# A hybrid decoder layer: the norm weights' row loaded first, one filter ordered behind scans, small products regrouped by array shape

## The chip, the cores and the metric

One core of a Trainium2 chip runs the whole program. The core has five engines that work at the same time and wait for each other by semaphores: TensorE (PE in the profile, its weight loads PEld), VectorE (DVE), ScalarE (ACT), GpSimd (POOL) and SyncE (SP), which here only issues DMA transfers. The metric is the device time of one execution in microseconds; the number given for a kernel is the median of its runs. Three runs of the kernel before took 1643.97, 1646.79 and 1654.39 us.

## The reference

One inference step of one decoder layer, for a prompt of 1024 positions and for 8 x 8 = 64 sample tokens; D_MODEL is 1024. All is in float32. The input projection feeds three groups of heads whose outputs are concatenated:

```python
h = rmsnorm(x, lw['g_mix'])
proj = h @ lw['w_in']
p_rw, p_cv, p_sb = jnp.split(proj, [RW_PROJ, RW_PROJ + 3 * CONV_DIM], axis=-1)
...
# recurrence (4 heads of 64), state s is 64 x 64 for each head
sa = jnp.einsum('bhvk,bhk->bhv', s, a_t)
s = (s * w_t[:, :, None, :] + sa[..., None] * b_t[:, :, None, :]
     + v_t[..., None] * k_t[:, :, None, :])
y = jnp.einsum('bhvk,bhk->bhv', s, r_t)
...
# short convolution, a filter of three taps
u = pc * px
ext = jnp.concatenate([conv_prev.astype(u.dtype), u], axis=1)
y = conv_w[0] * ext[:, 0:T]
for j in range(1, CONV_K):
    y = y + conv_w[j] * ext[:, j:j + T]
return pb * y, ext[:, -(CONV_K - 1):]
...
# stick-breaking attention (8 heads of 64)
log_beta = jnp.where(mask, jax.nn.log_sigmoid(z), -jnp.inf)
log_keep = jnp.where(mask, jax.nn.log_sigmoid(-z), 0.0)
later = lax.cumsum(log_keep, axis=3, reverse=True) - log_keep
wts = jnp.exp(log_beta + later)
...
x = x + mixed @ lw['w_out']
h2 = rmsnorm(x, lw['g_mlp'])
x = x + jnp.square(jax.nn.relu(h2 @ lw['w_up'])) @ lw['w_down']
gate = jax.nn.sigmoid(rmsnorm(x, lw['g_ple']) @ lw['w_ple_gate'])
x = x + gate * (p @ lw['w_ple_proj'])
```

The outputs also hold the new keys and values, the recurrence's final states, the last projection rows and the last two convolution inputs, for the prompt and for the samples.

## The kernel before

The code is one function that is traced from top to bottom. A planner then writes the order of each engine's instructions: it plays the program through with costs of its own, and takes at every engine the first instruction in program order that is ready in that play. So a line that stands earlier in the program has precedence, but does not always come first. Two calls restrict the planner: `tc.keep_in_program_order(x)` holds an instruction to its place in the program on its engine, and `with tc.issue_after(y)` puts what is traced inside it behind the instruction `y` on `y`'s engine. On the chip each engine and each DMA queue runs its list strictly in order. Buffers are named slots: `bufs=n` says how many tiles of a name live at once, and a tile that takes a used slot waits for the slot's last reader.

A float32 matrix product is split in two: a value is cast to a rounded format (fp32r, "hi"), the rest is kept as "lo", and three products of the parts are added. The recurrence and the transposes use plain float32, and each plain float32 product stands as two records in the profile.

**Stage 1, norm and transposes (lines 94 to 218, up to 38 us).** `x_tile` (L106) loads x in nine tiles of up to 128 rows through six slots. The row of norm weights (`gbc`, L113, 4 KB) is spread over 128 partitions by a product with ones (L120) and copied back (L121). For each tile: sum of squares (ACT, L205), root (L206), reciprocal (DVE, L208), scaling by it and the weights (DVE, L209), eight transposes (PE, L214), cast (ACT, L216), remainder (DVE, L217). The first input weights `w_da` are loaded before this loop; their casts are on ACT (L156) and their remainders on POOL (L159). Eleven rows of parameters (`prow`, L200) are loaded from POOL's queue; L223 transposes them into `par`, and L353 uses them. SP also carries small loads: `wl2` (L308 to L310), `sh` (L319), `gains` and `gainT` (L328, L330), `bias` (L791).

**Stage 2, recurrence inputs (to 150 us).** `rw_tile` makes the projections of the recurrence by `gemm_t` (L171 to L173, chunks of 384, 384 and 320 positions) and prepares products for its chunks of 64 positions.

**Stage 3, recurrence beside attention's projections (150 to 420 us).** Two streams of `wkv_local` work on pairs of chunks (`e` is 0 or 1, the chunk in the pair). L535 multiplies, for each `e`, `j` and half `s` of the partitions, a 64 x 128 stationary block by 128 columns; `s` 0 and 1 write two banks. Later products in it (L559 to L600) have 64 x 64 blocks. `wkv_chain` takes the pairs in order: L648 and L656 have 128 x 64 blocks and do not need the state; L659 and L665 have 64 x 64 blocks and need the state of the chunk before. For each chunk it goes L656, L659 for the first two heads, then L656, L659 for the other two, then L665. All of these lie between the dense products of the attention's projections (L898) and of the convolution (L171 to L173), which fill PE.

**Stage 4, samples, convolution and attention's first half (420 to 545 us).** `wkv_sample_chunk` does the samples' recurrence. `convolution` makes three projections; between the second and the third, for each half `j` of its columns, the filter runs as one ACT instruction (L1049) and two DVE instructions over 1104 columns (L1050, L1052). The third projection's result is multiplied by the filter's result as it leaves its bank (L1069); it has two banks. `attention` makes units, each a head and 256 queries: scores (PE, L954, L955), two sigmoids (ACT, L956, L957), masks (POOL, L961), scan (DVE, L963), product (DVE, L965), transposes (L979) and values (L983). Convolution and attention are traced in turns, five steps of the one and four of the other; `marks[1]` is the scan traced last.

**Stage 5, output projection, MLP, gate (545 us to the end)** is not touched.

## Time and profile before

| | |
|---|---|
| median of three runs | 1646.79 us |
| profiled execution | 1648.17 us |
| its span, first to last instruction | 1646.5 us |
| PE busy | 1617.9 us (98%) |
| DVE busy | 988.6 us (60%) |
| ACT busy | 774.2 us (47%) |
| POOL busy | 713.8 us (43%) |

The profiled execution is 1.4 us above the median. A line of the timeline has the start in us, the length in us of a group of like instructions, the engine, the line of the code, the operation, its output and inputs, their shapes, and the number of records. In square brackets stand idle time before it and what ended that. A matmul's length reaches into the next one's, since matmuls are pipelined, so that for PE the distance from one start to the next says more than the length. A row of windows has for each stretch the busy time of PE, PEld, DVE, ACT and POOL with the count of instructions, then the granted clock of PE and the DMA share.

### The profile page before, as it was taken

The page shows a single profiled execution, that of the slowest core. Times are in us where ns is not written, and L with a number is a line of the kernel's source. Part 1 is how long each engine was busy: PE and PEld are TensorE (multiplying, and loading weights), DVE is VectorE, ACT ScalarE, POOL GpSimd, SP SyncE. Part 2 cuts the span into 40 slices and gives each one's busy share as a digit, 9 for nine tenths or more (in the row PEclk, how much of TensorE's full clock was granted, in tenths as well). Part 3 has the DMA queues.
Part 4 walks back from the last instruction along what each step waited for, and adds up shares of the span by engine and source line. Part 5 has one row for each costly group of instructions (what it writes and reads, how often), then busy time and mean ns, then how long its engine had stood idle before and what let it go on. Part 6 is the DMA issues. An engine that isn't in the chain of part 4 may idle for free.

```text
span 1646.5 us, 28968 instructions
## 1 busy us (share of the span) xinstructions
PE 1617.9 (98%) x11215; PEld 1402.2 (85%) x11215; DVE 988.6 (60%) x1692; ACT 774.2 (47%) x1502; POOL 713.8 (43%) x793
## 2 busy tenths in 40 slices
PE   6999999999999999999999999999999999999998
PEld 5999777778976777777777789979999999999897
DVE  6367644554467698776344462478776777768332
ACT  7643245333356676665444452474433433437321
POOL 6321202232354664444256614467644554539110
PEclk9999999999999999999999999999999999999999
DMA  5245555434436534332356662223322222223211
GB/s 173 92 134 162 152 134 148 107 101 118 128 111 195 170 99 136 105 109 80 100 185 206 179 208 89 79 65 104 102 90 90 87 81 90 91 78 95 69 47 42
DMA packets 188148, 190.60 MB, mean 116 GB/s; under 512 B 57450, under 2 KB 147338, under 8 KB 187884
## 3 DMA queue, kind: packets, MB, share of 16 engines
q1 hardware_dynamic: 173644, 165.37, 33.6%
q0 software_dynamic: 5472, 16.81, 3.4%
q10 hardware_dynamic: 8896, 6.59, 1.6%
q8 instruction: 88, 1.44, 0.4%
q14 instruction: 48, 0.39, 0.1%
HBM read 154.09 MB, written 34.63 MB: 115 GB/s over the span
## 4 chain that ended last, share of the span: by engine, by line
PE 86%; DVE 6%; DMA 3%; POOL 2%; ACT 2%; issue 1%; SPq 0%; ACTq 0%; POOLq 0%; DVEq 0%
PE b L1140 13%; PE b L1141 13%; PE b L1142 13%; PE b L898 8%; PE b L171 3%; PE b L172 3%; PE b L173 3%; PE b L1498 3%; PE b L1499 3%; PE b L1497 3%; PE b L983 2%; PE b L979 2%; PE b L535 1%; DVE keep L963 1%; DMA wr<-in_w_up 1%
## 5 line engine op out<-in xcount | busy, mean ns | idle before, releaser
L1121 POOL TENSOR_TENSOR wl<-wr,wh 128x512 fp32r<-128x512 f32 x138 | 196.8, 1432 | 230.8 <-ACT wh L1120 227.5
L1541 DVE TENSOR_TENSOR x<-b,x 128x288 f32<-128x288 f32 (+1 forms) x384 | 199.1, 529 | 109.2 <-PE b L1142 107.6
L1120 ACT CAST wh<-wr 128x512 fp32r<-128x512 f32 x234 | 143.4, 621 | 218.0 <-PE b L1141 173.1
L1140 PE MATMUL b<-ah,wh 128*128 128x288 f32 (+1 forms) x612 | 202.6, 332 | 3.1 <-DVE x L1541 2.1
L1141 PE MATMUL b<-al,wh 128*128 128x288 f32 (+1 forms) x612 | 200.7, 328 | 0.2 <-POOL al L1511 0.2
L1142 PE MATMUL b<-ah,wl 128*128 128x288 f32 (+1 forms) x612 | 200.3, 328 | 0.0
L1140 PE MATMUL b<-nh,wh 128*128 128x512 f32 (+1 forms) x352 | 129.8, 369 | 0.3 <-DVE x L1452 0.2
L1141 PE MATMUL b<-nl,wh 128*128 128x512 f32 (+1 forms) x352 | 129.8, 369 | 0.0
L1142 PE MATMUL b<-nh,wl 128*128 128x512 f32 (+1 forms) x352 | 129.3, 367 | 0.0
L1140 PEld LDWEIGHTS b<-ah,wh 128*128 128x128 f32 x612 | 114.9, 188 | 13.8 <-DVE x L1541 3.8
L1141 PEld LDWEIGHTS b<-al,wh 128*128 128x128 f32 x612 | 115.0, 188 | 9.8 <-issue 1.7
L1142 PEld LDWEIGHTS b<-ah,wl 128*128 128x128 f32 x612 | 114.9, 188 | 7.9
L171 PE MATMUL b<-h_hi,wh 128*128 128x384 f32 (+1 forms) x336 | 114.3, 340 | 1.9 <-ACT xs L353 1.1
L963 DVE TENSOR_TENSOR_SCAN keep<-keep,onesq 128x128 f32<-128x128 f32 (+3 forms) x64 | 93.0, 1455 | 35.7 <-POOL keep L961 35.0
L172 PE MATMUL b<-h_lo,wh 128*128 128x384 f32 (+1 forms) x336 | 112.2, 334 | 1.0 <-DVE h_lo L217 1.0
L173 PE MATMUL b<-h_hi,wl 128*128 128x384 f32 (+1 forms) x336 | 111.9, 333 | 0.0
L1121 POOL TENSOR_TENSOR wsl<-s,wsh 128x512 fp32r<-128x512 f32 x60 | 77.3, 1308 | 25.7 <-ACT wsh L1120 25.7
L1121 DVE TENSOR_TENSOR wl<-wr,wh 128x512 fp32r<-128x512 f32 x96 | 76.0, 794 | 18.3 <-ACT wh L1120 17.6
L159 POOL TENSOR_TENSOR wl<-wr,wh 128x512 fp32r<-128x512 f32 x40 | 56.5, 1428 | 59.3 <-ACT wh L156 53.3
L898 PE MATMUL b<-wh,h_hi 128*128 128x512 f32 x192 | 78.0, 407 | 0.0
L898 PE MATMUL b<-wl,h_hi 128*128 128x512 f32 x192 | 76.2, 397 | 0.0
L898 PE MATMUL b<-wh,h_lo 128*128 128x512 f32 x192 | 76.1, 397 | 0.0
(483 smaller groups left out, 4446.1 us busy)
## 6 DMA issues: line engine op xcount, KB each, us to landing
wr<-in_w_up SPq DMA_DIRECT2D x64, 512.0 KB
wr<-in_w_down SPq DMA_DIRECT2D x64, 512.0 KB
wr<-in_w_in SPq DMA_DIRECT2D x26, 512.0 KB
wr<-in_w_out SPq DMA_DIRECT2D x16, 512.0 KB
xt<-in_x_prompt SPq DMA_DIRECT2D x8, 512.0 KB
stk_s<-sth ACTq DMA_DIRECT2D x32, 128.0 KB
stk_s<-stl SPq DMA_DIRECT2D x32, 128.0 KB
stk_q<-stk_s SPq DMA_DIRECT2D x16, 256.0 KB
```

The costliest lines, as they stand in the source:

```text
L159: sub[k0 // step % 2].tensor_sub(lo, raw[:, c:c + 512], f(hi))
L171: PE.matmul(ps[:, :n], wh[k][:, c], a, start=(k == 0), stop=False)
L172: PE.matmul(ps[:, :n], wh[k][:, c], b, start=False, stop=False)
L173: PE.matmul(ps[:, :n], wl[k][:, c], a, start=False, stop=(k == nk - 1))
L898: last = PE.matmul(ps[i], x[:, t0:t0 + 128], wt, start=start, stop=stop)
L963: marks[1] = V.tensor_tensor_scan(keep[:, 0:L][:, ::-1], keep[:, 0:L][:, ::-1], onesq[:, 0:1].to_broadcast([128, L]), 1.0, op0=ALU.mult, o ...
L1120: S.copy(h3, src)
L1121: (sub or G).tensor_sub(l3, src, f(h3))
L1140: PE.matmul(ps[:, :n], w(0, k, m), a, start=(k == 0), stop=False)
L1141: PE.matmul(ps[:, :n], w(0, k, m), b, start=False, stop=False)
L1142: PE.matmul(ps[:, :n], w(1, k, m), a, start=False, stop=(k == nk - 1))
L1541: V.tensor_add(p.x[:, m, t0:t0 + n], ps[:, :n], p.x[:, m, t0:t0 + n])
```

## The change

1. **Loads and order at the start.** The row of norm weights is asked for ahead of the x tiles. Each tile's reciprocal (L208) is put behind the spread's last copy (L121). `w_da` is traced after two tiles instead of ahead of all; its four casts go from ACT to DVE, and two of its four remainders from POOL to DVE. The parameter rows are traced behind the loop. The small loads of SP (`wl2`, `sh`, `gains`, `gainT`, `bias`) are held to their place in program order.
2. **L535 by shape.** For the prompt, each product with a 64 x 128 block becomes two with 64 x 64 blocks, in the order (s, a) = (0, 0), (1, 1), (0, 1), (1, 0), where `a` is the half of the block's columns. The samples keep the old form.
3. **Chain, chunk by chunk.** For each chunk the four products of L656 come first, then the four of L659. Accumulation in the bank is begun once by the first chunk's first two heads and ended by the last chunk's last two.
4. **Samples' buffers.** The slots named `um` become three; `bmk` shares them, and both `bmk` are made ahead of the two products of L763.
5. **Filter behind scans.** L1050 and L1052 are put behind `marks[1]`.

```diff
-    xts = [x_tile(0)]
     SP.dma_start(gbc[:1], bass.AP(tensor=gm.tensor, offset=gm.offset, ap=[[D, 1], [1, D]]))
-    xts += [x_tile(i) for i in range(1, 3)]
+    xts = [x_tile(i) for i in range(3)]
...
-        V.tensor_copy(gbc[:, g * 512:g * 512 + 512], pt)
+        spread = V.tensor_copy(gbc[:, g * 512:g * 512 + 512], pt)
...
-                    cast = S.copy(hi, raw[:, c:c + 512])
+                    made = cast(hi, raw[:, c:c + 512])
...
-    w_da = w_cols(768)
-    xts += [x_tile(i) for i in range(3, 6)]
     for i in range(9):
-        if i + 6 < 9:
-            xts.append(x_tile(i + 6))
         if i == 2:
-            for name, n in rows:
-                src = I[name]
-                G.dma_start(prow[at:at + n, :], bass.AP(tensor=src.tensor, offset=src.offset, ap=[[128, n], [1, 128]]))
+            w_da = W.load(w_in[:, 768:1024], cast=V.tensor_copy, sub=(G, V))
+            xts += [x_tile(n) for n in range(3, 6)]
...
-        V.reciprocal(rs[:r], st[:r, 1:2])
+        with tc.issue_after(spread.ins):
+            V.reciprocal(rs[:r], st[:r, 1:2])
...
+        if 2 <= i < 5:
+            xts.append(x_tile(i + 4))
     xpool.release()
+    for name, n in rows:
+        src = I[name]
+        G.dma_start(prow[at:at + n, :], bass.AP(tensor=src.tensor, offset=src.offset, ap=[[128, n], [1, 128]]))
...
-    SP.dma_start(wl2[:, 2], I["g2"][0])
+    tc.keep_in_program_order(SP.dma_start(wl2[:, 2], I["g2"][0]))
...
-                        PE.matmul(p4s[s][:, e, j, :], bk[hs, e, j].rearrange("p a t -> p (a t)"), ra,
-                                  start=True, stop=True)
+                        if sample:
+                            PE.matmul(p4s[s][:, e, j, :], bk[hs, e, j].rearrange("p a t -> p (a t)"), ra,
+                                      start=True, stop=True)
+                    for s, a in () if sample else ((0, 0), (1, 1), (0, 1), (1, 0)):
+                        hs = slice(64 * s, 64 * s + 64)
+                        ra = ar[hs, e, j, 0:2] if e == 0 else ar[hs, e, j, 2:0:-1]
+                        PE.matmul(p4s[s][64 * a:64 * a + 64, e, j, :], bk[hs, e, j, a], ra, start=True, stop=True)
...
-            for j in range(2):
-                for h in (2 * j, 2 * j + 1):
-                    PE.matmul(p4[hp(h), e, j, :], UV[:, e, h, :], AB[:, e, h, 64:128], start=True, stop=St is None)
-                if St is not None:
-                    for h in (2 * j, 2 * j + 1):
-                        PE.matmul(p4[hp(h), e, j, :], St[hp(h), j, :], Rm[hp(h), e, j, :], start=False, stop=True)
+            for h in range(4):
+                PE.matmul(p4[hp(h), e, h // 2, :], UV[:, e, h, :], AB[:, e, h, 64:128], start=e == 0 and h < 2,
+                          stop=False)
+            if St is not None:
+                for h in range(4):
+                    PE.matmul(p4[hp(h), e, h // 2, :], St[hp(h), h // 2, :], Rm[hp(h), e, h // 2, :], start=False,
+                              stop=e == 1 and h >= 2)
...
-                um = sp.tile([128, NB, 64], F32, name="um", tag="um", bufs=2)
+                um = sp.tile([128, NB, 64], F32, name="um", tag="um", bufs=3)
...
-                bmk = sp.tile([64, NB, 64], F32, name="bmk", bufs=1)
+                bmk = sp.tile([128, NB, 64], F32, name="bmk", tag="um", bufs=3)[0:64]
                 V.tensor_mul(bmk, AB[0:64, 0, h, None, 0:64].to_broadcast([64, NB, 64]), bm[0:64])
+                bmks.append(bmk)
+            for h, bmk in zip((2 * j, 2 * j + 1), bmks):
                 PE.matmul(pf[hp(h), :], Wm[0:64, h, :], bmk.rearrange("p b k -> p (b k)"), start=True, stop=True)
...
-    SP.dma_start(bias[:, 0], bass.AP(tensor=src.tensor, offset=src.offset, ap=[[0, 128], [1, 8]]))
+    tc.keep_in_program_order(SP.dma_start(bias[:, 0], bass.AP(tensor=src.tensor, offset=src.offset,
+                                                              ap=[[0, 128], [1, 8]])))
...
-            V.scalar_tensor_tensor(y[:, 0:LW - 2], u[:, 1:LW - 1], P1("conv_w", 2 + j), y[:, 0:LW - 2],
-                                   op0=ALU.mult, op1=ALU.add)
-            V.scalar_tensor_tensor(y[:, 0:LW - 2], u[:, 0:LW - 2], P1("conv_w", j), y[:, 0:LW - 2],
-                                   op0=ALU.mult, op1=ALU.add)
+            for i in (1, 0):
+                with tc.issue_after(marks[1].ins):
+                    V.scalar_tensor_tensor(y[:, 0:LW - 2], u[:, i:LW - 2 + i], P1("conv_w", 2 * i + j),
+                                           y[:, 0:LW - 2], op0=ALU.mult, op1=ALU.add)
```

More of the change, by code (lines that the diff above doesn't have):

```diff
@@ L143, in __init__, with load @@
             self.pool = pool
-        def load(self, src, nk=8, ncol=256, sub=(G, G), w=None, rows=None, pin=False):
+        def load(self, src, nk=8, ncol=256, sub=(G, G), w=None, rows=None, pin=False, cast=S.copy):
             w = w or ([], [])
@@ L155, in load @@
                     hi, lo = (self.pool.tile([128, 512], F32R, name=f"w{e}", bufs=8) for e in "hl")
-                    cast = S.copy(hi, raw[:, c:c + 512])
+                    made = cast(hi, raw[:, c:c + 512])
                     if pin:
-                        tc.keep_in_program_order(cast)
+                        tc.keep_in_program_order(made)
                     sub[k0 // step % 2].tensor_sub(lo, raw[:, c:c + 512], f(hi))
@@ L178, in hybrid_step @@
     V0 = SB0 + 1024
-    def w_cols(c0):
-        return W.load(w_in[:, c0:c0 + 256])
     rows = (("mu_shift", 8), ("w0", 2), ("a0", 2), ("k_k", 2), ("k_a", 2), ("r_k", 2), ("gn_w", 2), ("gn_b", 2),
@@ L318, in hybrid_step @@
     sh = pe_tile("sh")[:8, :1024]
[L319 removed]
+    tc.keep_in_program_order(SP.dma_start(sh, I["state_shift"][0]))
     pt = tr()
@@ L327, in hybrid_step @@
         src = I[name]
[L328 removed]
+        tc.keep_in_program_order(SP.dma_start(gains[:, n], bass.AP(tensor=src.tensor, offset=src.offset,
+                                                                   ap=[[0, 128], [1, 64]])))
         for s in range(2):
[L330 to L331 removed]
+            tc.keep_in_program_order(SP.dma_start(gainT[64 * s:64 * s + 64, n:n + 1],
+                                                  bass.AP(tensor=src.tensor, offset=src.offset,
+                                                          ap=[[1, 64], [1, 1]])))
     reset = rp.tile([128, T], F32, name="reset")
@@ L727, in wkv_sample_chunk @@
             pt = bank()
-            s_in = sp.tile([128, NB, 64], F32, name="s_in", tag="um", bufs=2)
+            s_in = sp.tile([128, NB, 64], F32, name="s_in", tag="um", bufs=3)
             for s in range(2):
@@ L779, in wkv_sample_chunk @@
                     PE.matmul(po[hs, b * 64:b * 64 + 64], GS[hs, b, :], ident[hs, hs], start=True, stop=True)
-            so = sp.tile([128, NB, 64], F32, name="so", tag="um", bufs=2)
+            so = sp.tile([128, NB, 64], F32, name="so", tag="um", bufs=3)
             S.copy(so.rearrange("p b k -> p (b k)"), po)
```

16 lines of the change are left out of this document (6 added, 10 removed).

## The prediction

> **What bounds the kernel now.** I read the page first (engines, chain), then busy time by window, then the timeline of each engine at the places that the change touches.
>
> ```profile
> span 1646.5 us, 28968 instructions
> PE 1617.9 (98%) x11215; PEld 1402.2 (85%) x11215; DVE 988.6 (60%) x1692; ACT 774.2 (47%) x1502; POOL 713.8 (43%) x793
> PE 86%; DVE 6%; DMA 3%; POOL 2%; ACT 2%; issue 1%; SPq 0%; ACTq 0%; POOLq 0%; DVEq 0%
> 0.00:20.00 20.00, 9.56 (x34) 6.79 (x35) 10.92 (x16) 14.64 (x30) 17.06 (x34) 0.98 0.70 234
> 20.00:40.00 20.00, 17.99 (x111) 16.28 (x109) 14.13 (x26) 13.08 (x29) 8.87 (x28) 0.94 0.46 122
> 250.00:300.00 50.00, 50.00 (x464) 39.91 (x463) 24.77 (x54) 22.23 (x47) 12.74 (x12) 1.00 0.53 139
> 460.00:465.00 5.00, 3.97 (x32) 3.69 (x32) 4.40 (x9) 2.20 (x7) 3.56 (x7) 0.78 0.49 154
> ```
>
> TensorE is busy for 98% of the span and carries 86% of the chain that ended last. So two things shorten this kernel: PE time that disappears where PE has no gap, and the 28.6 us (1646.5 - 1617.9) in which PE stands. Of these 12.45 us lie in the first 40 us (40 - 9.56 - 17.99). From 250 to 300 us, in the recurrence, PE has no gap: there only fewer PE nanoseconds count. From 460 to 465 us PE stands for 1.0 us, and its clock was granted at 0.78.
>
> **The start (edit 1).**
>
> ```profile
> 0.81 0.39 SPq L106 DMA_DIRECT2D xt<-in_x_prompt  x1
> 1.27 0.31 SPq L113 DMA_DIRECT2D gbc<-in_g_mix  x1
> 4.86 3.75 PE L120 MATMUL b<-gbc,onesq 1*128 1x512 f32 x4 [4.86 <-DMA gbc<-in_g_mix]
> 8.99 0.67 DVE L121 COPY gbc<-b 128x512 f32<-128x512 f32 x1
> 10.36 3.68 DVE L209 SCALAR_TENSOR_TENSOR xt<-xt,rs,gbc 128x1024 f32<-128x1024 f32 x3
> 17.70 1.10 SPq L330 DMA_DIRECT2D gainT<-in_k_gain  x2
> 18.93 0.50 SPq L106 DMA_DIRECT2D xt<-in_x_prompt  x1
> 23.87 1.06 ACT L205 ACTIVATE junk<-xt 128x1024 f32<-128x1024 f32 x1 [2.40 <-DMA xt<-in_x_prompt]
> 25.38 0.17 DVE L208 RECIPROCAL rs<-st 128x1 f32<-128x1 f32 x1 [2.18 <-ACT st L206]
> 10.23 1.14 ACT L156 CAST wh<-wr 128x512 fp32r<-128x512 f32 x2
> 31.99 1.26 DVE L217 TENSOR_TENSOR h_lo<-b,h_hi 128x512 fp32r<-128x512 f32 x2
> 37.55 0.41 PE L172 MATMUL b<-h_lo,wh 128*128 128x320 f32 x1 [0.73 <-DVE h_lo L217]
> ```
>
> The spread (L120) waits for the weights' row, which was queued behind an x tile. Ahead of it, the row lands earlier by 0.46 us at least (the distance of the two issues) and by 0.46 plus the tile's own transfer at most: 512 KB at the first window's 234 GB/s are 2.2 us. I take 1.8, so that the spread ends at 7.9 instead of 9.66 us. The x tiles land up to 0.46 us later, which the spread covers. The seventh tile was asked for at 18.93, right behind the small loads (17.70 is the last of them), although the slot of the first tile was free soon after its scaling (three take 3.68 us from 10.36). Held in order, the small loads go behind it: it can be asked for some 4 us earlier, and the wait for it (ACT at 23.87, then DVE with 2.18 us of idle time) goes. What is late next is DVE itself. A tile costs it 3.68/3 for L209, 0.17 and 1.26 for L208 and L217, 2.66 in all and 23.9 for nine. The edit adds four casts and two remainders. DVE's cast of this form isn't in the trace; ACT's takes 0.57 (1.14 for two), DVE's copy of it from a bank 0.67. I take 0.6 and 0.63 for a remainder (half of 1.26): 3.7 us more. From 7.9, 27.6 us end at 35.5; PE stood until 37.55 for the last remainder. That is -2.0, with -3.5 where DVE's overlaps are better and +1.5 where the row comes only 0.46 earlier and DVE idles as before. From there PE has no gap that this could vanish in. The small loads now queue behind three x tiles on SP; at half a microsecond of issue each (two in 1.10) twelve of them are out some 7 us after the last tile, at about 24 us by estimate, and their readers stand behind the loop. The parameter rows move behind the loop on POOL and may come after its two remainders; they too are read behind the loop only. I cost both at nothing: what hides them is DVE's work up to 35.5. Without that cover PE stands as long as the latest of them is late.
>
> `bias`, held in order, comes behind the recurrence's outputs:
>
> ```profile
> 421.38 0.51 DVE L792 TENSOR_SCALAR bias<-bias 128x8 f32<-128x8 f32 x1
> 421.50 2.41 SPq L712 DMA_DIRECT2D out<-St  x4
> ```
>
> DVE multiplies it at 421.38; the load now starts at 423.9 at the earliest, so DVE waits at least 2.5 us (423.91 - 421.38), with what is queued behind it, the normalisation of the last chunk and the products that free the convolution's banks. PE has a chunk of work in the other bank; I take 0, at most +1.
>
> **The chain by chunk (edit 3).**
>
> ```profile
> 283.37 0.34 PE L656 MATMUL b<-AB,UV 128*64 128x64 f32 x4
> 283.63 0.33 PE L659 MATMUL b<-Rm,St 64*64 64x64 f32 x4
> 283.80 0.40 PE L665 MATMUL b<-St,FT 64*64 64x64 f32 x8
> 284.13 0.34 PE L656 MATMUL b<-AB,UV 128*64 128x64 f32 x4
> 371.42 0.65 PE L600 MATMUL b<-AB,Wm 64*64 64x128 f32 x8
> 372.00 1.16 PE L535 MATMUL b<-ar,bk 64*128 64x128 f32 x8
> 373.09 0.33 PE L659 MATMUL b<-Rm,St 64*64 64x64 f32 x4
> 288.02 0.27 PE L659 MATMUL b<-Rm,St 64*64 64x64 f32 x1
> 288.02 0.37 PE L600 MATMUL b<-AB,Wm 64*64 64x128 f32 x2
> ```
>
> By starts, four records of L656 (128x64 blocks) take 0.26 us, and the twelve of L659 and L665 (64x64) that follow take 0.50. Eight more records cost 0.24, so 0.03 each; four are 0.12, and 0.14 is left for the change of block shape. The edit merges L656, L659, L656, L659 into L656, L659 for each chunk that has a state: 15 of 16, two changes less in each, 30 x 0.14 = 4.2 us, on PE where it has no gap. No instruction is added. Bounds: 0 if the planner puts dense products between, 5 if the chain's shorter latency helps as well.
>
> **L535 by shape (edit 2).** A half of it (one s) has eight records and takes 1.09 us (372.00 to 373.09): 0.14 for the shape and 0.12 a record, one after the other. The new form is L600's, a 64x64 block by 128 columns: eight records in 0.58 (371.42 to 372.00), 0.055 each besides the shape, since two blocks run at once. Twice as many records are 0.14 + 16 x 0.055 = 1.02 us, 0.07 less, for 16 halves 1.1 us. And at the sides where L535's neighbour has 64x64 blocks, as at both ends of the run at 372.00, no change of shape is left; along the timeline these are 12 sides from 227.96 to 373.09, 12 x 0.14 = 1.7:
>
> ```profile
> 227.96 1.16 PE L535 MATMUL b<-ar,bk 64*128 64x128 f32 x8
> ```
>
> Together -2.8. Against this speaks a rule. The Trainium skill, TensorE: Matmul & The Clock Gate, section Packing small matmuls, says that a weight load overlaps a running matmul only where the two use different row groups. The two blocks of one half s lie in one row group, so by the rule they run one after the other; the sum would be the slow rival's below. L600 speaks against the rule: a run of eight records is one chunk, one row half, and its two column halves ran together.
>
> **Samples' buffers (edit 4).**
>
> ```profile
> 489.57 1.08 PE L759 MATMUL b<-um,AB 128*64 128x512 f32 x4
> 492.50 1.07 PE L763 MATMUL b<-bmk,Wm 64*64 64x512 f32 x2
> 511.74 1.07 PE L759 MATMUL b<-um,AB 128*64 128x512 f32 x2
> 513.59 1.07 PE L759 MATMUL b<-um,AB 128*64 128x512 f32 x2 [0.42 <-DVE um L756]
> ```
>
> Two products of L759 together took 1.08 us; where the second had to wait for a slot (513.59, 0.42 us behind DVE) they took 1.07 each. L763 runs four times alone; as two pairs at 1.08 it saves 2 x 1.07, and the second pair of L759 one more: -3.2, and up to -3.6 with the wait. Added: a `bmk` now waits for a shared slot; -2 if that parts one pair again.
>
> **The filter (edit 5).**
>
> ```profile
> 435.62 1.37 DVE L1050 SCALAR_TENSOR_TENSOR cc<-ue,par,cc 128x1104 f32<-128x1104 f32 x1 [1.41 <-ACT cc L1049]
> 457.21 1.34 DVE L1050 SCALAR_TENSOR_TENSOR cc<-ue,par,cc 128x1104 f32<-128x1104 f32 x1
> 459.46 1.35 DVE L1052 SCALAR_TENSOR_TENSOR cc<-ue,par,cc 128x1104 f32<-128x1104 f32 x1
> 460.74 1.61 DVE L963 TENSOR_TENSOR_SCAN keep<-keep,onesq 128x256 f32<-128x256 f32 x2
> 462.86 0.69 PE L171 MATMUL b<-h_hi,wh 128*128 128x384 f32 x1 [0.17 <-DVE cc L1069]
> ```
>
> Before, the first half's filter ran at 435.62 on an idle DVE, and the second half's stood at 457.21 and 459.46 ahead of the scans at 460.74. Now the first goes behind the scan traced last, the first of the two at 460.74, and the second behind a scan four units later. Around 458 one filter so takes the other's place on DVE, but behind the scan, which comes up to 2.7 us (1.34 + 1.35) earlier. Who waits for that: attention's transposes and the next sigmoids. Who pays: L1069, queued behind the filter, frees the bank for which PE stood at 462.86. I take -1.5 (one us of the standing and half a us of clock); -5 if the low clock of this window goes too, +4 if the bank comes 2.7 us later and the clock falls again. Here a second rule: the Trainium skill, same page, section HAM oscillation, names idle gaps over about 3.4 us as what slows the clock. No gap here is that long, and the clock fell to 0.78. By the rule the edit can't win clock back; by this row it can. Without the half microsecond of clock the sum would be 0.5 less.
>
> **The sum.** -2.0 - 4.2 - 2.8 - 3.2 - 1.5 = -13.7. The profiled execution took 1648.17 (span 1646.5 and 1.7 around it) and lies 1.4 above the median of 1646.79; so 1634.5 for a run like it, and 1633 against the median.
>
> **The rivals.**
> - *Forecast, 1633* (1626 to 1641): 0.52. For it: each larger term is PE time in a stage without a gap.
> - *More runs at once.* At 288.02 two records of L600 and one of L659 start together, three blocks in the array. If the four blocks of both halves s meet in the queue, 32 records take 1.02 instead of 2.18 us; for eight pairs of chunks that is 8 x 1.02 = 8 us more than above: 1625. Against it: the two halves mostly stand microseconds apart (227.96, and the next run of it only after dense products). 0.15.
> - *Half is lost at the filter.* What the recurrence saves is given back at 455 to 465 us, where DVE and not PE ends the wait, half of the chain's and L535's 7.0, and the filter is at its bound: -2.0 - 3.5 - 3.2 + 4 = -4.7, so 1642. For it: PE stands there already, and each queue but PE's keeps its pace. 0.23.
> - *Slower: the new blocks run one by one.* Then a half is 0.14 + 16 x 0.12 = 2.06 us instead of 1.09; 16 halves are +15.5, less 1.7 for the sides: +13.8. The other edits give -10.9, so 1650. It decides once some 100 of the 128 added records find nothing to overlap with. Against it L600's pairs; for it the rule above. 0.10.
>
> **How the numbers follow.** The likeliest case gives 1633. The range takes in 1625 with one microsecond of the start's bounds and goes up to the slow rival, 1622 to 1650; below lie the first rival's better half of bounds (0.07), above it the slow rival's worse half and an unlucky order of the planner (0.08). Within 1%, about what a measurement tells from no change, is 1630.3 to 1663.3. Faster by more: the 0.15 of the first rival and somewhat over a quarter of the forecast's 0.52, 0.29 together. Slower by more needs the slow rival and the filter's bound together: 0.03. The rest, 0.68.
>
> **What would show it.** Start: L120 near 3 us, the seventh tile's transfer asked for before 15 us, the last remainder of the loop before 36.5. Chain: L656 and L659 in runs of eight; none of four between. L535: 64x64 runs of sixteen records in about 1.0 us, not 2. Samples: L763 in two runs of four records. Filter: the window around 460 with PE over 4.5 us busy of 5 and a clock near 1. Wrong I would be if runs of L535 lasted 2 us, if PE's gap before 40 us grew beyond 12.45 us, or if the windows between 440 and 520 us had more idle PE than before.

## The result and the profile after

The changed kernel took 1635.36 us, the median of five runs (1632.47 to 1635.87), against 1646.79 (1643.97 to 1654.39) for the kernel before: a ratio on record of 0.9917, with a 95% interval of 0.9896 to 0.9939; the two medians alone are 11.4 us apart, which is 0.9931. Forecast were 1633.0 with 1622 to 1650. So the time was met; the terms behind it were not all met, as the following shows. The profiled execution took 1632.47 us, the shortest of the five, so the two profiles lie further apart (15.7 us) than the medians.

The page of the changed kernel (span, busy times, chain of waits):

```profile
span 1630.7 us, 29223 instructions
PE 1599.8 (98%) x11343; PEld 1392.4 (85%) x11343; DVE 991.3 (61%) x1698; ACT 771.3 (47%) x1498; POOL 703.6 (43%) x791
PE 85%; DVE 6%; DMA 4%; ACT 2%; POOL 2%; issue 1%; SPq 0%; ACTq 0%; DVEq 0%; POOLq 0%
```

The span is 15.8 us shorter, and PE's busy time 18.1 us. PE's standing time grew from 28.6 to 30.9 us. All of the gain is therefore PE time that is no longer needed. Its windows, in the order that the prediction used:

```profile
0.00:20.00 20.00, 10.94 (x33) 7.50 (x34) 14.13 (x23) 14.64 (x30) 16.89 (x51) 0.93 0.85 294
20.00:40.00 20.00, 19.11 (x118) 17.75 (x116) 14.25 (x25) 12.06 (x26) 4.75 (x8) 0.90 0.23 56
250.00:300.00 50.00, 48.56 (x516) 38.18 (x514) 29.37 (x58) 22.00 (x46) 13.84 (x14) 1.00 0.55 142
460.00:465.00 5.00, 5.00 (x71) 4.09 (x67) 4.05 (x7) 2.11 (x6) 3.33 (x7) 1.00 0.03 11
```

The row from 460 to 465 us holds other work than before, since this stage now comes some 14 us earlier; it is taken up again below.

In the first 40 us PE now stands for 9.95 us (40 - 10.94 - 19.11) instead of 12.45, but its granted clock is 0.93 and 0.90 instead of 0.98 and 0.94. What is left of this is read from the product with which the attention's projections begin, in the timeline of the kernel before and then of the changed one:

```profile
146.59 0.39 PE L898 MATMUL b<-wh,h_hi 128*128 128x512 f32 x1
```

```profile
146.17 0.39 PE L906 MATMUL b<-wh,h_hi 128*128 128x512 f32 x1
```

In this pair of traces the start has won 0.42 us. From there to the end of the recurrence the changed kernel wins another 13.0 us (the products that turn its last states for output start at 407.29 instead of 420.68), up to the first product of the MLP's second matrix 3.7 more (614.39 instead of 631.51), and it loses 1.4 us in two stands behind 1120 us: 15.7 in all.

The start, in the timeline of the changed kernel (its L119 is L120 of before, L155 is L156, L171 is L172, L207 is L217, L316 is L319):

```profile
2.50 3.75 PE L119 MATMUL b<-gbc,onesq 1*128 1x512 f32 x4 [2.50 <-DMA gbc<-in_g_mix]
10.07 0.80 DVE L155 CAST wh<-wr 128x512 fp32r<-128x512 f32 x2
12.59 2.30 DVE L155 CAST wh<-wr 128x512 fp32r<-128x512 f32 x2
18.70 0.69 PE L171 MATMUL b<-h_lo,wh 128*128 128x384 f32 x1 [3.41 <-DVE h_lo L207]
36.24 0.63 DVE L207 TENSOR_TENSOR h_lo<-b,h_hi 128x256 fp32r<-128x256 f32 x1
40.30 0.48 SPq L316 DMA_DIRECT2D sh<-in_state_shift  x1
```

The spread begins 2.4 us earlier. But DVE then has the four casts, and PE stands 3.41 us for a remainder that is queued behind them.

The recurrence, in the timeline of the changed kernel (L540 is the new form of L535, L659 and L663 are L656 and L659 of before):

```profile
200.97 0.67 PE L540 MATMUL b<-ar,bk 64*64 64x128 f32 x16
280.39 1.09 PE L540 MATMUL b<-ar,bk 64*64 64x128 f32 x16
287.54 1.37 PE L540 MATMUL b<-ar,bk 64*64 64x128 f32 x32
363.48 1.04 PE L540 MATMUL b<-ar,bk 64*64 64x128 f32 x29
364.26 0.39 PE L663 MATMUL b<-Rm,St 64*64 64x64 f32 x6
364.82 0.45 PE L659 MATMUL b<-AB,UV 128*64 128x64 f32 x8
```

The run at 280.39 takes 1.02 us (the next product starts at 281.41). By the patterns of its moving operands it holds eight records of each of the two chunks, so I take it for one half s: its records start in pairs 6 to 8 ns apart, a pair every 0.11 us. The run at 200.97 has records of the first chunk alone, so it holds both halves: four start within 20 ns, 0.16 and then 0.11 us behind the four ahead of them, and sixteen take 0.60 us. At 287.54 and at 363.3, where both halves had gathered in the queue, 32 records take 1.30 and 0.93 us. At 364.3 the chain's products follow in the same way, eight of L659 for a chunk in one run.

The groups of PE by line, from 195 to 560 us: total busy time and mean ns of one record, first of the kernel before, then of the changed one:

```profile
L535 PE MATMUL b<-ar,bk 64*128 64x128 f32 x136 | 19.8, 290 | 0.0
L656 PE MATMUL b<-AB,UV 128*64 128x64 f32 x128 | 12.0, 242 | 0.0
L659 PE MATMUL b<-Rm,St 64*64 64x64 f32 x112 | 10.0, 240 | 0.0
```

```profile
L540 PE MATMUL b<-ar,bk 64*64 64x128 f32 x256 | 15.1, 276 | 0.0
L535 PE MATMUL b<-ar,bk 64*128 64x128 f32 x8 | 1.4, 297 | 0.0
L659 PE MATMUL b<-AB,UV 128*64 128x64 f32 x128 | 8.2, 231 | 0.0
L663 PE MATMUL b<-Rm,St 64*64 64x64 f32 x112 | 7.3, 227 | 0.0
```

Nearly twice as many records of L535's work cost less. Since busy times reach into the next record, I count PE's time below by starts: from each record to the next, without standing time, summed by line.

The samples and the filter, in the timeline of the changed kernel (L764 is L759 of before, L770 is L763, L987 is L979, L1060 is L1050 and L1052, L800 is L792):

```profile
417.16 0.17 DVE L800 TENSOR_SCALAR bias<-bias 128x8 f32<-128x8 f32 x1 [4.02 <-DMA bias<-in_sb_bias]
443.94 0.69 DVE L971 TENSOR_TENSOR_SCAN keep<-keep,onesq 128x256 f32<-128x256 f32 x1
444.54 1.34 DVE L1060 SCALAR_TENSOR_TENSOR cc<-ue,par,cc 128x1104 f32<-128x1104 f32 x1
446.36 0.44 PE L987 MATMUL b<-ident,beta 128*128 128x128 f32 x2 [1.17 <-DVE beta L973]
497.01 1.08 PE L764 MATMUL b<-um,AB 128*64 128x512 f32 x4
501.64 1.07 PE L770 MATMUL b<-bmk,Wm 64*64 64x512 f32 x2
503.80 1.07 PE L770 MATMUL b<-bmk,Wm 64*64 64x512 f32 x2
```

The filter stands behind a scan. Around it PE still stands: 1.17 us ahead of the transposes at 446.36 and 0.34 at 444.75. The products of L759 run in pairs; one of the two pairs of L763 still runs apart.

### The profile page after: what moved, and what is told of

Read it like the earlier page. It is cut to its first block, busy times and chain, and to the rows that moved or that the text cites. A ratio compares the mean times of both kernels' runs of the same rounds, so it can differ in the third digit from the quotient of the medians.

```text
span 1630.7 us, 29223 instructions
## 1 busy us (share of the span) xinstructions
PE 1599.8 (98%) x11343; PEld 1392.4 (85%) x11343; DVE 991.3 (61%) x1698; ACT 771.3 (47%) x1498; POOL 703.6 (43%) x791
## 3 DMA queue, kind: packets, MB, share of 16 engines
q1 hardware_dynamic: 173644, 165.37, 33.6%
## 4 chain that ended last, share of the span: by engine, by line
PE 85%; DVE 6%; DMA 4%; ACT 2%; POOL 2%; issue 1%; SPq 0%; ACTq 0%; DVEq 0%; POOLq 0%
PE b L1148 14%; PE b L1149 14%; PE b L1150 14%; PE b L906 8%; PE b L170 3%; PE b L171 3%; PE b L1506 3%; PE b L1507 3%; PE b L1505 3%; PE b L172 3%; PE b L991 2%; PE b L987 2%; DMA wr<-in_w_up 1%; PE b L1273 1%; DMA wr<-in_w_out 1%
## 5 line engine op out<-in xcount | busy, mean ns | idle before, releaser
L1129 POOL TENSOR_TENSOR wl<-wr,wh 128x512 fp32r<-128x512 f32 x138 | 196.0, 1425 | 235.6 <-ACT wh L1128 234.5
L171 PE MATMUL b<-h_lo,wh 128*128 128x384 f32 (+1 forms) x336 | 113.0, 336 | 3.4 <-DVE h_lo L207 3.4
L172 PE MATMUL b<-h_hi,wl 128*128 128x384 f32 (+1 forms) x336 | 112.0, 334 | 0.0
L158 POOL TENSOR_TENSOR wl<-wr,wh 128x512 fp32r<-128x512 f32 x38 | 52.0, 1382 | 64.5 <-ACT wh L155 60.0
L1148 PEld LDWEIGHTS b<-nh,wh 128*128 128x128 f32 x352 | 66.2, 188 | 12.2 <-DVE x L1460 2.6
```

The source lines that it names most:

```text
L158: sub[k0 // step % 2].tensor_sub(lo, raw[:, c:c + 512], f(hi))
L171: PE.matmul(ps[:, :n], wh[k][:, c], b, start=False, stop=False)
L172: PE.matmul(ps[:, :n], wl[k][:, c], a, start=False, stop=(k == nk - 1))
L1129: (sub or G).tensor_sub(l3, src, f(h3))
L1148: PE.matmul(ps[:, :n], w(0, k, m), a, start=(k == 0), stop=False)
```

## The experiments

The experiments ran on three other chips. There the kernel before took 1667 to 1670 us, so only ratios to the kernel before on the same chip are compared. Where this comes from is seen in the first of them.

### The kernel before on another chip

No edit.

> The kernel before, unchanged, for its trace beside those of the other kernels on one chip. Theory A (the loss of the single edits lies in the convolution and the first half of attention): between 420 and 600 us PE stands some 5 us (5.1 in the first trace), against 10.7 and 10.9 with edit 2 or edit 3 alone. Theory B (the loss is this chip's, in the cached attention around 800 to 950 us, and hits every kernel alike): PE stands 10 to 11 us there in this kernel too if the chip is the same, and none of the differences between kernels comes from there. Both can be true; if PE's stand between 420 and 600 is 10 here too, A falls.

Measured: 1670.97 us, beside a median of 1667.86 for other runs of the same kernel there. The window from 800 to 1000 us of this run, and then of the first profile of the same kernel:

```profile
800.00:1000.00 200.00, 188.19 (x1242) 142.81 (x1241) 82.27 (x118) 79.25 (x148) 90.85 (x89) 0.97 0.54 165
```

```profile
800.00:1000.00 200.00, 200.00 (x1343) 155.44 (x1342) 91.92 (x130) 89.64 (x164) 97.46 (x94) 1.00 0.58 177
```

PE stands 11.8 us and has a lower clock (0.03 x 200 = 6 us at most, since it stood for part of that time) in the cached attention, which the change does not touch. Both theories of the expectation held: in this window all kernels on these chips stand for 9.8 to 12.6 us, and between 420 and 600 us this kernel stands for 4.6 us, near the 5.1 of the first trace.

### L535 by shape alone

The kernel before, with edit 2 and nothing else.

```diff
-                        PE.matmul(p4s[s][:, e, j, :], bk[hs, e, j].rearrange("p a t -> p (a t)"), ra,
-                                  start=True, stop=True)
...
+                    for s, a in () if sample else ((0, 0), (1, 1), (0, 1), (1, 0)):
...
+                        PE.matmul(p4s[s][64 * a:64 * a + 64, e, j, :], bk[hs, e, j, a], ra, start=True, stop=True)
```

> The kernel before with edit 2 alone (L535's products by shape). Measure: the time from the first small product of the recurrence to the last product of the attention's projections (175.75 us in the kernel before, 165.49 in the changed one), and the distances between starts over a run of L535's new form. Theory A (four blocks at once): where both halves s stand in the queue, runs of 32 records take some 1.3 us, and of 16 between 0.6 and 1.0; the stretch is 5 to 6 us shorter, and the time about 1641. Theory B (the forecast's price: two blocks at once, 1.02 us for 16 records): the stretch is 2.8 us shorter and the time about 1644; what the changed kernel gained beyond that then comes from the chain. Theory C (one by one): the stretch is some 14 us longer, 1660.

Measured: 1670.63 us, a ratio of 1.0025 (1.0015 to 1.0036). None of the theories: the edit alone makes the kernel slower by 4 us. The stretch that the expectation named takes 176.03 us, as long as before.

### The chain chunk by chunk alone

The kernel before, with edit 3 and nothing else.

```diff
-            for j in range(2):
-                for h in (2 * j, 2 * j + 1):
-                    PE.matmul(p4[hp(h), e, j, :], UV[:, e, h, :], AB[:, e, h, 64:128], start=True, stop=St is None)
...
+            for h in range(4):
+                PE.matmul(p4[hp(h), e, h // 2, :], UV[:, e, h, :], AB[:, e, h, 64:128], start=e == 0 and h < 2,
+                          stop=False)
...
```

> The kernel before with edit 3 alone (the chain, chunk by chunk). Same stretch, 175.75 us before and 165.49 after. Forecast's price: 30 changes of block shape less, 4.2 us, time about 1642.5. Rival 1 (records of L656 and L659 also run closer together in runs of eight, as the changed kernel's trace has them: 10.6 us by starts instead of 16.0): 5.4 us less and about 1641. Rival 2 (it needs edit 2 beside it, because the runs join only when both have 64x64 blocks): at most 2 us less, 1645.

Measured: 1668.40 us, a ratio of 1.0006 (0.9996 to 1.0017). Again no gain, although the named stretch, at 165.37 us, is as short as in the changed kernel. From the first small product to the last one that needs a state (L665) it is the other way round: 204.3 us with the shape alone, 212.6 with the chain alone, 214.0 before. So the dense products among the small ones stand elsewhere in these kernels, and neither stretch measures what an edit saves.

### Both together

The kernel before, with the two diffs above and nothing else of the change.

> The kernel before with edits 2 and 3 together, without 1, 4 and 5. Theory A (given back behind the recurrence): the PE time of L535, L648, L656, L659, L665 and L600 falls by about 13 us as in the changed kernel, but between 420 and 600 us PE stands 9 us or more and the granted clock falls there; ratio 0.996 to 1.000. Theory B (the two edits lose only when alone, because the runs join only when both are in): PE stands at most 6.5 us between 420 and 600, ratio 0.992 to 0.994.

Measured: 1655.55 us, a ratio of 0.9918 (0.9901 to 0.9936). That is as much as the whole change gains. Theory B of the expectation is right in its numbers: the stand between 420 and 600 us is 4.8 us. But its reason is not what happened, as PE's time by starts shows (us, sums over the prompt and the samples; "before" is the run on the second chip; "stand" is PE's standing time from 420 to 600 us):

| | before | shape alone | chain alone | both | changed kernel |
|---|---|---|---|---|---|
| L535 | 18.3 | 15.1 | 17.3 | 13.2 | 13.2 |
| L656 and L659 | 16.0 | 15.5 | 12.3 | 10.6 | 10.6 |
| L600, L648, L665 | 20.2 | 17.9 | 19.2 | 17.4 | 17.5 |
| sum | 54.6 | 48.5 | 48.8 | 41.2 | 41.3 |
| stand | 4.6 | 10.7 | 10.9 | 4.8 | 6.5 |

In the recurrence the two edits are nearly additive: 6.1 and 5.8 us alone, 13.4 together. Alone, each loses its gain behind the recurrence. The windows of that stage for the kernel before on the second chip, shape alone, chain alone, and both:

```profile
420.00:600.00 180.00, 175.37 (x1181) 140.99 (x1180) 120.39 (x163) 104.58 (x213) 99.79 (x163) 0.98 0.49 147
```

```profile
420.00:600.00 180.00, 169.28 (x1138) 136.18 (x1137) 116.66 (x153) 101.63 (x204) 90.97 (x163) 0.94 0.50 150
```

```profile
420.00:600.00 180.00, 169.07 (x1145) 132.30 (x1144) 121.67 (x160) 104.70 (x208) 98.37 (x164) 0.96 0.50 146
```

```profile
420.00:600.00 180.00, 175.24 (x1160) 138.04 (x1159) 126.42 (x163) 111.92 (x222) 95.77 (x158) 0.97 0.48 147
```

Alone, each edit has 6 us more of standing PE, and the clock is 0.94 and 0.96 instead of 0.98; without the time in which PE stood anyway, that costs 5.5 and 3.6 us more than before. What PE waits for there, by the waits of shape alone and then of chain alone, is attention's own work and the output projection's transposes:

```profile
PE b L988 <- ACT wt L986: 3.2, 1, 3.2
PE b L959 <- ACT keep L962: 2.6, 1, 2.6
PE b L984 <- DVE beta L970: 2.5, 1, 2.5
PE b L1354 <- DVE x L1357: 2.0, 1, 2.0
```

```profile
PE b L955 <- ACT keep L958: 4.5, 3, 2.6
PE b L1350 <- DVE x L1353: 2.0, 1, 2.0
```

The planner wrote another order for this stage in these two kernels. With both edits its order of PE behind the recurrence is almost that of the kernel before: of the first 1200 groups of like products there, 98% stand in the same order, with the shape or the chain alone 41 and 36%. A mark of the other order is how far the samples' last product (L779 of before) starts behind the convolution's last one (L173): 35.3 and 49.4 us in the single edits, 28.7 and 28.8 in the kernel before and with both. Why the planner changed its order was not tested; that the order costs these stands is read from the traces, and no run holds the order fixed.

### The changed kernel with the start of before

The changed kernel, with all of edit 1 undone: the row behind the first x tile, `w_da` ahead of the loop with its casts on ACT, the small loads not held, and so on.

```diff
-    xts = [x_tile(i) for i in range(3)]
+    xts += [x_tile(i) for i in range(1, 3)]
...
+    w_da = w_cols(768)
+    xts += [x_tile(i) for i in range(3, 6)]
...
-            w_da = W.load(w_in[:, 768:1024], cast=V.tensor_copy, sub=(G, V))
...
-    tc.keep_in_program_order(SP.dma_start(sh, I["state_shift"][0]))
+    SP.dma_start(sh, I["state_shift"][0])
```

> The changed kernel with the start of the kernel before (edit 1 undone, the held small loads too). Theory from the two traces: edit 1 takes 2.5 us of idle PE out of the first 40 us and loses most of it again because PE then runs twice as long at the lower granted clock (0.71 and 0.61 in the windows 15-20 and 20-25, before 0.91 and 0.75), so the first product of the attention's projections stands at 146.6 us again (146.17 with edit 1) and the time is 0.4 us longer, 1635.8. The forecast's price for edit 1 would make it 2.0 longer, 1637.4. Rival: edit 1 changes the order further on too (the held loads), then milestones behind 150 us move by more than 0.5 us against each other.

Measured: 1653.97 us, a ratio of 0.9914 (0.9897 to 0.9930), with the attention's first product at 145.90 us. By the times, which can tell apart some 3 us, the start of before is as good as that of the change. A part of the reason is in the clock. In the first pair of traces the windows from 15 to 25 us were short of 1.7 us of clock before the change (clocks 0.91 and 0.75) and of 3.4 after it (0.71 and 0.61). In this run with the old start the clock did not fall at all, but the start as such is not the reason: in the six other traces with the same start (the kernel before twice, edits 2 and 3 alone and together, and both with the filter) it fell for 3.4 us each time. Over all traces, the attention's first product stands at 145.90 to 147.34 us with the old start (seven traces, mean 146.7) and at 144.90 to 146.51 with edit 1 (four, mean 145.9). So edit 1 is worth about 0.8 us, less than either start varies. The rival is not excluded: behind the recurrence the two kernels move by 2.2 us against each other (the first product of the MLP's second matrix is at 616.34 here and at 614.39 in the changed kernel), on different chips.

### The casts back on ACT

The changed kernel, with one line of edit 1 changed.

```diff
-w_da = W.load(w_in[:, 768:1024], cast=V.tensor_copy, sub=(G, V))
+w_da = W.load(w_in[:, 768:1024], cast=S.copy, sub=(G, G))
```

> The changed kernel, but the four casts of w_da on ACT and all four remainders on POOL as in the kernel before; all else of edit 1 stays. Theory: DVE's four casts and two remainders (some 4.4 us in the trace) push the remainders of the x tiles back, for which PE stands 3.41 us at 18.70, and that stand is what the lower clock follows. Without them the stand at that place falls under 1.5 us, PE's granted clock in 15 to 25 us rises, and the first product of the attention's projections comes 1.5 to 2.5 us earlier: time about 1633.5. Rival 1 (the late small load of the shift state, asked for at 40.3, sets the pace): no change at that product, 1635.4. Rival 2 (ACT is late instead, its squares and casts follow the weights): up to 1 us later, 1636.4.

Measured: 1651.68 us, a ratio of 0.9905 (0.9882 to 0.9927). The attention's first product stands at 144.15 us, 2.0 earlier than in the changed kernel, as the theory has it; a second trace of this start, in the last experiment, has 143.41. The stand at 18.70 for DVE's remainder is gone. But PE now stands 2.64 us for ACT's cast of an x tile, as the second rival feared, and the clock did not rise:

```profile
12.00:14.00 2.00, 0.67 (x6) 0.42 (x4) 1.21 (x2) 2.00 (x4) 1.92 (x3) 1.00 1.02 402
14.00:18.00 4.00, 2.54 (x7) 2.14 (x8) 3.25 (x6) 3.97 (x10) 4.00 (x4) 0.60 1.06 337
18.00:22.00 4.00, 4.00 (x18) 3.74 (x17) 3.93 (x7) 3.70 (x9) 3.91 (x9) 0.55 1.21 259
```

PE stood from 12.67 to 15.31 us and had half the clock from 14.8 us on for 6.8 us, as long as in the changed kernel.

### PE kept busy in that stand

The kernel with the casts on ACT, with 14 dead transposes behind the third tile's.

```diff
+        if i == 2:
+            fill = psum.tile([128, 512], F32, name="b2", bufs=1)
+            for _ in range(14):
+                with tc.issue_after(last_t.ins):
+                    PE.transpose(fill[:, 0:128], onesq, ident)
```

> The changed kernel with the casts of w_da on ACT, and with 14 transposes of constants, written to an unread bank, held behind the third tile's transposes, where PE stood from 12.67 to 15.31 us. Theory (the half clock from 14.9 to 21.7 us follows that stand of 2.64 us): with PE busy there the granted clock from 14 to 22 us is 1.00, and the first product of the attention's projections comes up to 3.4 us (half of 6.8) earlier than 144.15, at about 141.5, since DVE and ACT still have to deliver; ratio about 0.989. Rival 1 (the clock falls whatever PE does there, as it comes from the start of the program): the clock is 0.50 again for 3.4 to 6.8 us and the product stands at 144 or later. Rival 2 (the clock is held, but ACT and DVE set the pace): clock 1.00, the product within 0.5 us of 144.15, PE stands longer before 40 us.

Measured: 1651.95 us, a ratio of 0.9900 (0.9887 to 0.9912). Its windows:

```profile
14.00:18.00 4.00, 3.42 (x25) 2.93 (x24) 3.62 (x7) 3.93 (x10) 4.00 (x6) 1.00 1.04 320
18.00:22.00 4.00, 4.00 (x31) 3.96 (x30) 3.76 (x7) 4.00 (x11) 3.75 (x11) 1.00 1.22 269
22.00:26.00 4.00, 2.81 (x22) 2.34 (x21) 4.00 (x6) 3.69 (x9) 3.61 (x7) 1.00 0.38 68
```

The clock is whole, and the attention's first product comes at 142.22, 1.2 and 1.9 us earlier than in the two traces without the filling and 4.0 earlier than in the changed kernel. The times do not show it: the ratio is 0.9905 and 0.9894 without the filling. Not the full 3.4 us of half clock come back: from 22 to 26 us PE now stands 1.2 us for DVE and ACT, which are busy for nearly all of that window. So the lower clock did follow PE's stand in this start, and both the theory and its second rival have a part.

### Without the filter edit

The changed kernel with edit 5 undone.

```diff
-            for i in (1, 0):
-                with tc.issue_after(marks[1].ins):
-                    V.scalar_tensor_tensor(y[:, 0:LW - 2], u[:, i:LW - 2 + i], P1("conv_w", 2 * i + j),
...
+            V.scalar_tensor_tensor(y[:, 0:LW - 2], u[:, 1:LW - 1], P1("conv_w", 2 + j), y[:, 0:LW - 2],
...
+            V.scalar_tensor_tensor(y[:, 0:LW - 2], u[:, 0:LW - 2], P1("conv_w", j), y[:, 0:LW - 2],
...
```

> The changed kernel without edit 5 (the filter where it was). Theory A (the filter behind the scans is what lets the recurrence's gain through): between 420 and 600 us PE stands 9 us or more, and the time is 4 to 10 us longer than the changed kernel's 0.9917 of before: ratio 0.994 to 0.998. Forecast's price for edit 5, 1.5 us: ratio 0.9926. Rival (edit 4 or the order of the planner does it, not the filter): ratio 0.991 to 0.992.

Measured: 1652.76 us, a ratio of 0.9905 (0.9888 to 0.9921). The rival is right: the filter behind the scans does not carry the gain. In this kernel it is worth nothing that can be measured. PE stands 7.0 us from 420 to 600 us here, against 6.5 in the changed kernel.

### Without the samples' buffers

The changed kernel with edit 4 undone.

```diff
-                um = sp.tile([128, NB, 64], F32, name="um", tag="um", bufs=3)
+                um = sp.tile([128, NB, 64], F32, name="um", tag="um", bufs=2)
...
-                bmk = sp.tile([128, NB, 64], F32, name="bmk", tag="um", bufs=3)[0:64]
+                bmk = sp.tile([64, NB, 64], F32, name="bmk", bufs=1)
...
-                bmks.append(bmk)
-            for h, bmk in zip((2 * j, 2 * j + 1), bmks):
...
```

> The changed kernel without edit 4 (two slots for um, bmk alone). Forecast's price 3.2 us: ratio 0.9936. From the changed kernel's trace: L763 lost 1.0 and L759 1.1 us of PE time by starts, so 2.1 us, ratio 0.993, and the stand between 420 and 600 us grows by under 1 us. Rival (the shared slots let the samples' recurrence run ahead and fill PE where the convolution stands): the stand grows by 3 us or more and the ratio is 0.995 to 0.997.

Measured: 1660.43 us, a ratio of 0.9950 (0.9933 to 0.9966). The rival is right in its numbers: PE stands 11.1 us from 420 to 600 us, 4.6 more. The largest wait of that stage is not the convolution's but one for `bmk`:

```profile
PE b L768 <- DVE bmk L767: 4.3, 1, 4.3
```

### Shape, chain and filter, without start and samples' buffers

The kernel before, with the diffs of edits 2, 3 and 5.

```diff
+            for i in (1, 0):
+                with tc.issue_after(marks[1].ins):
+                    V.scalar_tensor_tensor(y[:, 0:LW - 2], u[:, i:LW - 2 + i], P1("conv_w", 2 * i + j),
...
```

> The kernel before with edits 2, 3 and 5, without 1 and 4. Theory A (the filter behind the scans costs unless the samples' buffers are changed with it: with 1, 2, 3 and 5 the ratio was 0.995, with 2 and 3 alone 0.9918): PE stands 8 us or more between 420 and 600 us, the samples' last product comes over 35 us behind the convolution's last one, ratio 0.995 to 0.997. Theory B (the filter costs nothing; the loss with 1, 2, 3 and 5 came from an order that edit 1 had moved): PE stands about 5 us there and the ratio is 0.991 to 0.992.

Measured: 1663.07 us, a ratio of 0.9959 (0.9946 to 0.9971), against 0.9918 without the filter edit: the filter costs 6.8 us here (0.0041 x 1668, give or take 3.6 by the two intervals, which are from two chips). Theory A is right. PE stands 9.7 us from 420 to 600 us, and the samples' last product comes 40.7 us behind the convolution's. In the timelines, first of PE, then of DVE, one stand is seen at its place:

```profile
522.52 1.97 PE L769 MATMUL b<-bmk,Wm 64*64 64x512 f32 x2 [3.06 <-DVE bmk L768]
```

```profile
515.17 0.96 DVE L969 TENSOR_TENSOR_SCAN keep<-keep,onesq 128x384 f32<-128x384 f32 x1 [1.40 <-POOL keep L967]
516.90 2.28 DVE L969 TENSOR_TENSOR_SCAN keep<-keep,onesq 128x512 f32<-128x512 f32 x1 [0.19 <-POOL keep L967]
520.73 1.74 DVE L768 TENSOR_TENSOR bmk<-AB,bm 64x512 f32<-64x512 f32 x1
```

The second `bmk` waits for its single slot and then stands behind scans on DVE; PE waits for it. This stand is 3.06 of the 4.9 us that PE stands longer than without the filter edit. The rest is not traced to one wait, and PE's order is another here too (50% of the groups as in the kernel before, 42% in the kernel without edit 4, 78% in the changed one), so that not all of the loss is shown to be `bmk`'s. In the changed kernel both are made ahead of the products. So edit 4 is needed because of edit 5: with both or with neither the ratio is 0.991 to 0.992, with edit 4 and no filter edit 0.9905, with the filter edit and no edit 4 0.995 to 0.996.

### The changed kernel, and a version of it, on a third chip

First the changed kernel as it is, then with the casts of `w_da` on ACT and edit 5 undone (the diffs of these two stand above).

> The changed kernel itself, beside the other three on one chip. If this chip stands in the cached attention around 800 to 950 us as the chip of the last runs did (10 to 12 us of PE), this kernel loses them too, and its ratio stays near 0.9917; PE's stand between 420 and 600 us is again 6.5 us.

> The changed kernel with the casts of w_da on ACT and without edit 5. Theory: the casts on ACT are worth some 2 us (the first product of the attention's projections at 144.2 against 146.2 us), the filter behind the scans is worth nothing, so the ratio is about 0.990 and 1.5 to 3 us below the changed kernel's. Rival (the two do not add up: the order behind the recurrence falls differently and PE stands 8 us or more between 420 and 600): ratio 0.993 or more.

Measured: 1654.32 us, ratio 0.9911 (0.9893 to 0.9930), for the changed kernel; 1651.04 us, ratio 0.9894 (0.9879 to 0.9908), for the other. The attention's first product stands at 146.51 and at 143.41 us. The second kernel's 3.1 us at the start are plain in the traces; by the times, whose intervals overlap, the two are not separated. The stand from 420 to 600 us is 7.8 and 7.3 us: the changed kernel's is 1.3 more than in its first trace and than was expected.

## Why the prediction was right, and where it was not

**The sum.** Forecast were -13.7 us; the ratio on the first chip is -13.7 us as well (0.0083 x 1646.79, interval -10.0 to -17.1), the medians are 11.4 us apart, and the ratio on another chip agrees. But that the sum comes out is luck: two errors cancel. Edits 2 and 3, forecast at -7.0, bring all of it, 13.4 us of PE time; edits 1, 4 and 5, forecast at -6.7, bring nothing that the times can tell, which is some 3 us either way for each ratio. By the traces edit 1 is worth about 0.8 us, and edit 4 saves 2.1 us of PE time.

**L535 by shape (forecast -2.8).** The mechanism, two blocks at once and no change of shape at the sides, was right and the term too small: L535 lost 5.1 us by starts, 3.2 with the shape alone, where the forecast had 1.1, and its neighbours lost more. I priced all 16 halves at two blocks at once, 1.02 us, and this is what a lone half takes (280.39). The rival "more runs at once" was the truth wherever both halves stood in the queue, at 0.9 to 1.3 us for 32 records; my reason against it, that the halves mostly stand apart, was read from the old order of work, which the edit itself changes. The slow rival is refuted for these blocks: in the run at 280.39 the two column halves of one row half start 6 to 8 ns apart. The next weight loads begin 0.05 us behind the run's first two products and 0.10 us ahead of the next two, in a run that takes 0.11 us from pair to pair. So the rule that the Trainium skill has in "TensorE: Matmul & The Clock Gate", section Packing small matmuls, that a weight load overlaps only where the row groups differ, does not hold in this run, nor does what the prediction drew from it, that the blocks run one after the other.

**The chain (forecast -4.2).** L656 and L659 lost 5.4 us by starts, 3.7 with the chain alone. So alone, the forecast's price of 0.14 for a change of shape was nearly right; together with edit 2 the gain is above the bound of 5, which I took from changes of shape alone. L600, L648 and L665 lost 2.7 more, of which the forecast had the sides next to L535 (1.7, counted there). Blocks of 64 by 64 of different lines overlap as those of one line do, as at 364.3.

**Half lost at the filter (rival, 0.23).** The recurrence's gain was not given back in the changed kernel: 13.4 us ahead at the end of the recurrence, it is 17.1 ahead at the MLP's second matrix. The window from 460 to 465 us, which the prediction named, is no sign of this; the work that stood there before is at 444 to 451 us now. There PE stands 1.5 us (2.0 before), and the clock is again halved for 3.4 us, from 447.2 on. This rival names the very thing that makes each of edits 2 and 3 useless alone: each saves some 6 us of PE time and loses it to stands and clock behind the recurrence. I put the place at the convolution's bank; it was attention, the samples and the output projection.

**The start (forecast -2.0, measured -0.4 in the first pair of traces and -0.8 over all).** The step that failed is "DVE's work up to 35.5" as the only thing that counts. The last remainder came at 36.24, and PE's standing time did shrink by 2.5 us; but the sum lacks a term for PE's clock. At the halved clock PE worked 5.2 us (6.8 less 1.6 of standing) instead of 3.4, which costs 0.9 us. Ahead of the first record of the clock its transposes start every 0.213 us instead of 0.109; it worked 5.2 us at this rate instead of 3.9, which costs 0.7 more. The price of a cast on DVE, 0.6, was off both ways: 0.40 at 10.07, 1.15 at 12.59. The small loads were estimated at 24 us; the shift state was asked for at 40.30, since the loads held in order also stand behind a weight load that waits for its buffer. It cost PE 0.3 us: cost at nothing was nearly right, the reason was not. The order that I named as a sign, the seventh tile before 15 us, came true and did not matter.

**`bias` (forecast 0).** Right: DVE waits 4.02 us for it, and PE has no stand around it.

**Samples' buffers (forecast -3.2).** By starts L763 lost 1.0 and L759 1.1 us, since one pair stayed apart; the forecast named -2 for that case. What the term missed is that the edit undoes a wait for `bmk` which is there with the filter edit.

**The filter (forecast -1.5, bounds -5 to +4).** Wrong: without edit 4 it costs 6.8 us, in part through `bmk` behind the scans; beside edit 4 it brings nothing. Of the one us of standing and the half of clock that were forecast, 0.5 and nothing came.

## What to carry to other kernels

Small products of one block shape that are queued together are cheaper than their instruction count says: count the blocks that can share the array at once, over all lines that will stand next to each other, not within one line. Two edits that each save PE time can each be worth nothing alone when an order made by a planner follows them, so try them together before dropping either, and look for where the time reappears. A start with idle PE cost twice here, by the stand and by the clock after it; filling a stand with dead products brought 1.2 to 1.9 us of the start in the traces and nothing that the times could show. One trace of each of two starts is not enough to rank them when the same start varies by 1.4 us.

## What the hardware showed that was not expected

- **Blocks at once.** Four records of 64 x 64 blocks by 128 columns start within 20 ns of each other, mostly every 0.11 us (200.97, sixteen in 0.60 us); two from one row half start 6 to 8 ns apart in the same rhythm (280.39, sixteen in 1.02 us).
- **The clock.** In all 14 traces the granted clock changes only at whole multiples of 3.41 us from its other changes in the same trace; low stretches last 3.4, 6.8 or 10.2 us, but for the one that the program's end cuts off. Two such steps of the kernel before, the second halved:

```profile
15.66:19.07 3.41, 1.01 (x9) 0.80 (x9) 3.41 (x5) 3.41 (x9) 3.41 (x3) 1.00 0.12 22
19.07:22.49 3.42, 3.42 (x15) 3.42 (x14) 3.38 (x7) 1.71 (x4) 3.37 (x9) 0.50 0.37 109
```

  In the starts, up to 40 us, a fall followed each of the 12 steps at the whole clock in which PE stood 2.13 to 2.97 us, and none of those with 1.86 us or less. The low clock lasted a second step where PE stood 0.65 us or more in the first, and not where it stood 0.47 or less. So it is the standing within a step that counts there, and the steps lie otherwise in each run. The stand of 2.24 us in the run with the old start is parted by a border at 25.30 us into 1.43 and 0.81, and no fall followed. Two stands lie ahead of the first record of the clock (15.06 and 14.00 us): 2.94 us in that run and 2.27 with the filling. There the transposes start every 0.213 us instead of 0.109, so that PE ran at half its later rate already, although the rows of windows give 1.00. Behind 400 us falls came after less standing too, some after none (as behind the step from 473.0 us of the kernel before); why is open. In "TensorE: Matmul & The Clock Gate", section HAM oscillation, the Trainium skill names gaps over about 3.4 us; falls here followed gaps of 2.40 us (the kernel before) and 2.64 (casts on ACT).
- **A chip.** The kernel before took 1646.79 us on one chip and 1667 to 1670 on three others; in the profiles most of the difference lies in the cached attention, where PE stands 12 us and its clock is 0.97 over 200 us.
